# The SSD of a hybrid encoder trunk: decay as one exponent, states ahead of heads, no priority

## Chip, cores, metric

The kernel runs on one core of a Trainium2 chip. Its time is the device time of one execution in microseconds. The engines are named as the profile names them: PE (TensorE; PEld its weight loads), DVE (VectorE), ACT (ScalarE), POOL (GpSimd), and SP, which issues the DMAs.

## What is computed

A trunk of two layers on a sequence of L = 512 tokens and D = 1024 channels. Each layer normalises x, projects it, runs four mixers side by side (a bidirectional Mamba-2 SSD, a bidirectional RWKV-7 and two attentions), projects their 2048 channels back to 1024 and adds the result to x. The part that the change touches is the SSD, per direction:

```python
def _ssd(x, dt, A, bm, cm):
    xdt = chunk(x * dt[..., None])
    a = jnp.moveaxis(chunk(dt * A), -1, 1)
    a_cum = jnp.cumsum(a, axis=-1)
    scores = jnp.einsum("bclhn,bcshn->bhcls", cm, bm) * jnp.exp(_segsum(a))
    y_diag = jnp.einsum("bhcls,bcshp->bclhp", scores, xdt)
    decay_states = jnp.moveaxis(jnp.exp(a_cum[..., -1:] - a_cum), 1, -1)
    states = jnp.einsum("bclhn,bclhp->bchpn", bm, xdt * decay_states[..., None])
    ...
    y_off = jnp.einsum("bclhn,bchpn->bclhp", cm, states) * state_decay_out[..., None]
    return y_diag + y_off

y = y_f + y_b + xs * d_skip
```

There are 8 heads of 64 channels in two groups of four, which share B and C; chunks are of 128 tokens, so there are 4 of them and 3 state steps per direction. y is gated with silu(z) and normalised per group.

## The kernel before

`trunk` runs the layers one after the other. In a layer, `rwkv` runs first, with the attentions woven in. Then come the SSD (`ssd`), with work of others woven in, and the output projection, in two halves hf of 512 output channels. Projections are matmuls in three passes of high and low parts (whi·hhi, whi·hlo, wlo·hhi): a weight tile wf is loaded, ACT copies its high part (L153 in `split_w`), POOL subtracts for the low part (L154). `mm` (L82) issues every matmul, so PE's rows are told apart by tiles, not lines.

The names in `ssd`:

- The dt part works on 64 rows (2 directions of 32, of which 8 are heads). `sdt` is dt, `se` the running sum ac of dt·A within a chunk, `su` the decay to the chunk's end times dt (L738 to L747). Three PE transposes (pcx, L752) bring ac, dt and su into columns `colT` (L753); `exT` is exp(ac).
- `project(g)` makes, for group g, the convolved inputs: pjc (projection), craw (ACT L767), cacc (four DVE steps L772), cv (ACT tanh L774, DVE L775); then pjt for the gate zs; then transposes pxt to xs and bt (L793, L794) and pg to gT (L801), the product of C and B.
- Heads (L820 on): per head and direction, prow is a matmul that broadcasts ac over partitions; ACT takes four chunk ends, etot (L824); four DVE instructions subtract the column and take the minimum with a mask (L828); ACT takes exp (L831). Then per head 4 DVE products with dt (L837), 4 products with dt and sums (L838), one product with gT to mt (L841), and PE's yd, four matmuls. Two heads share one yd bank; ACT copies it to y (L849).
- States: three steps of POOL xd (L859), PE stp, and H on DVE (L864, or POOL L866 and DVE L869). Outputs: per chunk PE po, DVE of = po·exT (L881), POOL y += of (L884), POOL sk = xs·D (L888), DVE y += sk/2 (L890).
- Norm: y·zs (L893), squares jk on ACT (L897), rstd on DVE (L134) and POOL (L136), zs (L903).

The output projection adds 16 tiles kt of 128 mixer channels, 12 matmuls `mix` each per half. Kts 0 to 3 are the SSD's, 4 to 7 need no transposes, 8 to 15 are loaded (y) and transposed by PE (ytr L1251) into a "pj" bank, then split by ACT (yhi L1256) and DVE (ylo L1257). Weights are split at L1264 and L1265. The list `more` offers kts 4 to 15 of half 0 as fill work during group 1; kts 0 to 3 follow behind the SSD, and half 1 behind them.

What sets the order: the program is written in one order; a scheduler puts each engine's instructions in its own, by priority, which follows the program order, and `tc.high_priority()` raises everything issued while `urgent` is open. `with usual(): fill(...)` closes it for woven work. PSUM banks are 2 for "pj", 2 for "g" (pcx, prow, yd, stp, po, pxt, pg), 1 for "ga" and 3 for "mix".

Of the kernel before, what the change touches and what calls it, by code (L numbers as in the profile page):

```python
# [19 lines left out]
L = 512  # L20
# [11 lines left out]
F_S1 = 0.54  # L32
# [43 lines left out]
def trunk(ctx: ExitStack, tc: tile.TileContext, x_in, win, wwd, wdt, wout, w2a, cols, rows, sscal, consts, out, dbg=None,  # L76
# [4 lines left out]
    def mm(o, lhsT, rhs, start, stop, skip=False):  # L81
        PE.matmul(o, lhsT, rhs, start=start, stop=stop, skip_group_check=skip)  # L82
# [610 lines left out]
    def ssd(i, lay, ps, sp, op, yA, fill, more):  # L693
# [13 lines left out]
            G.tensor_tensor(w[:, :, 1, :], wf[:, h], w.bitcast(F32)[:, :, 0, :], op=ALU.subtract)  # L707
            ws.append(w.rearrange("p k a n -> p k (a n)"))
        fill.settle()
        urgent.enter_context(tc.high_priority())  # L710
        pd = ps.tile([128, L], F32, tag="pj", name="pjd")
        for k in range(8):
            mm(pd, ws[k // 4][:, k % 4, :], hT["hi"][:, k, :], k == 0, False)
# [31 lines left out]
                            op=ALU.subtract)  # L745
        S.activation(dec, dec, AF.Exp)
        V.tensor_tensor(dec, dec, dt, op=ALU.mult)  # L747
        colT = sp.tile([128, 3, 4, 64], F32, tag="colT", name="colT")
        for n, src in enumerate((ac, dt, dec)):
            pcx = ps.tile([128, 4, 64], F32, tag="g", name="pcx")  # L750
# [56 lines left out]
        for g in range(2):  # L807
            if g:
                fill.finish()
                fill.gens.extend(more)  # L810
            urgent.enter_context(tc.high_priority())
            cv, zs, xs, bt, gT = (gr[g][n] for n in ("cv", "zs", "xs", "bt", "gT"))

            etot = sp.tile([128, 2, 4, 4], F32, tag="etot", name="etot")
            y = sp.tile([128, 4, 256], F32, tag="y", name="y")
            yd = None
            for h in range(4):
                ex = []
                for d in range(2):
                    ri = d * 8 + 4 * g + h  # L820
                    pr = ps.tile([128, L], F32, tag="g", name="prow")
                    mm(pr, selE[:, ri:ri + 1].to_broadcast([128, 128]), acs, True, True)
                    p4 = pr.rearrange("p (c t) -> p c t", c=4)
                    S.activation(etot[:, d, :, h:h + 1], p4[:, :, 127:128] if d == 0 else p4[:, :, 0:1], AF.Exp)  # L824
                    ar = sp.tile([128, 4, 128], F32, tag="ar", name="ar", bufs=2)
                    row = 32 * d + 4 * g + h
                    for ch in range(4):
                        V.scalar_tensor_tensor(ar[:, ch, :], p4[:, ch, :], colT[:, 0, ch, row:row + 1],  # L828
                                               mneg[:, d * 128:d * 128 + 128],
                                               op0=ALU.subtract, op1=ALU.min)  # L830
                    S.activation(ar, ar, AF.Exp)  # L831
                    ex.append(ar)
                    with usual():
                        fill(F_S1)
                for ch in range(4):
                    row = 4 * g + h
                    V.tensor_scalar(ex[0][:, ch, :], ex[0][:, ch, :], colT[:, 1, ch, row:row + 1], None, op0=ALU.mult)  # L837
                    V.scalar_tensor_tensor(ex[1][:, ch, :], ex[1][:, ch, :], colT[:, 1, ch, row + 32:row + 33],  # L838
                                           ex[0][:, ch, :], op0=ALU.mult, op1=ALU.add)
                mt = sp.tile([128, 4, 128], F32, tag="mt", name="mt", bufs=2)  # L840
                V.tensor_tensor(mt, ex[1], gT, op=ALU.mult)  # L841
                with usual():
                    fill(F_S2)
                if h % 2 == 0:
                    yd = ps.tile([128, 4, 2, 64], F32, tag="g", name="yd")
                for ch in range(4):
                    mm(yd[:, ch, h % 2, :], mt[:, ch, :], xs[:, ch, h * 64:h * 64 + 64], True, True)
                if h % 2 == 1:
                    S.activation(y[:, :, (h - 1) * 64:(h + 1) * 64], yd.rearrange("p c h v -> p c (h v)"), AF.Copy)  # L849

            H = [[None] * 4, [None] * 4]
            for step in range(3):
                stp = ps.tile([128, 2, 256], F32, tag="g", name="stp")
                for d in range(2):
                    ch = step if d == 0 else 3 - step
                    nx = ch + 1 if d == 0 else ch - 1
                    row = 32 * d + 4 * g
                    xd = sp.tile([128, 4, 64], F32, tag="xd", name="xd", bufs=2)
                    G.tensor_tensor(xd, xs[:, ch, :].rearrange("p (h v) -> p h v", h=4),  # L859
                                    colT[:, 2, ch, row:row + 4].unsqueeze(2).to_broadcast([128, 4, 64]), op=ALU.mult)  # L860
                    mm(stp[:, d, :], bt[:, ch, :], xd.rearrange("p h v -> p (h v)"), True, True)
                    hn = sp.tile([128, 256], F32, tag=f"H{d}{step}", name="H")
                    if step == 0:
                        V.tensor_copy(hn, stp[:, d, :])  # L864
                    else:
                        G.tensor_tensor(hn.rearrange("p (h v) -> p h v", h=4),  # L866
                                        H[d][ch].rearrange("p (h v) -> p h v", h=4),
                                        etot[:, d, ch, :].unsqueeze(2).to_broadcast([128, 4, 64]), op=ALU.mult)
                        V.tensor_tensor(hn, hn, stp[:, d, :], op=ALU.add)  # L869
                    H[d][nx] = hn  # L870
                with usual():
                    fill(F_S3)
            for ch in range(4):
                po = ps.tile([128, 2, 256], F32, tag="g", name="po")
                ds = [d for d in range(2) if H[d][ch] is not None]
                for d in ds:
                    mm(po[:, d, :], cv[6 + g][:, ch * 128:ch * 128 + 128], H[d][ch], True, True)
                of = sp.tile([128, 2, 256], F32, tag="of", name="of", bufs=2)
                for d in ds:
                    row = 32 * d + 4 * g  # L880
                    V.tensor_tensor(of[:, d, :].rearrange("p (h v) -> p h v", h=4),  # L881
                                    po[:, d, :].rearrange("p (h v) -> p h v", h=4),
                                    exT[:, ch, row:row + 4].unsqueeze(2).to_broadcast([128, 4, 64]), op=ALU.mult)
                    G.tensor_tensor(y[:, ch, :], y[:, ch, :], of[:, d, :], op=ALU.add)  # L884
                with usual():
                    fill(F_S4)
# [12 lines left out]
            with usual():  # L899
                fill(F_S5)  # L900
# [453 lines left out]
def _consts():  # L1354
# [17 lines left out]
    c[:, C_MNEG + 128:C_MNEG + 256] = np.where(p[:, None] >= p[None, :], 0.0, -1e30)  # L1372
# [102 lines left out]
```

## Time and profile before

| | |
|---|---|
| median of 3 runs | 1831.52 us (1824.56 to 1835.34) |
| the profiled execution | 1831.36 us |
| its span | 1829.6 us |
| PE, DVE, ACT, POOL busy | 88%, 61%, 45%, 38% of the span |
| first mix matmul of half 0 to the last, layer 1 | 745.1 to 870.3 us |

The profile is of one execution; times count from the start of its span. A busy share is a share of time in which the engine has an instruction in work, and PE counts as busy at half clock as well; the granted clock of a stretch stands in the windows' column PEclk, 1.00 being 2.4 GHz.

### The profile page before, as it was taken

The page shows a single profiled execution, that of the slowest core. Times are in us where ns is not written, and L with a number is a line of the kernel's source. Part 1 is how long each engine was busy: PE and PEld are TensorE (multiplying, and loading weights), DVE is VectorE, ACT ScalarE, POOL GpSimd, SP SyncE. Part 2 cuts the span into 40 slices and gives each one's busy share as a digit, 9 for nine tenths or more (in the row PEclk, how much of TensorE's full clock was granted, in tenths as well). Part 3 has the DMA queues.
Part 4 walks back from the last instruction along what each step waited for, and adds up shares of the span by engine and source line. Part 5 has one row for each costly group of instructions (what it writes and reads, how often), then busy time and mean ns, then how long its engine had stood idle before and what let it go on. Part 6 is the DMA issues. An engine that isn't in the chain of part 4 may idle for free. (4 is left out here: it accounts for less than half of the span.)

```text
span 1829.6 us, 36888 instructions
## 1 busy us (share of the span) xinstructions
PE 1606.7 (88%) x15232; PEld 1347.2 (74%) x15232; DVE 1109.3 (61%) x2130; ACT 819.4 (45%) x1602; POOL 694.2 (38%) x708
## 2 busy tenths in 40 slices
PE   7898989998999979956988989899989999699478
PEld 6777877887878858844777777678778787588356
DVE  3567477486566357754256765865866763677632
ACT  4655436436435354521347463264274353554222
POOL 4554334243434125233455443342425251343223
PEclk9999988998999989976999999899979999899679
DMA  4211101110101132300431111011101010323013
GB/s 148 79 64 38 46 15 62 36 36 31 53 24 48 48 104 81 122 23 35 132 102 63 64 34 48 24 50 33 50 13 65 30 59 31 107 79 115 12 46 121
DMA packets 57512, 108.50 MB, mean 59 GB/s; under 512 B 6784, under 2 KB 8704, under 8 KB 57344
## 3 DMA queue, kind: packets, MB, share of 16 engines
q1 hardware_dynamic: 57344, 106.15, 17.4%
q8 instruction: 119, 1.95, 0.4%
q14 instruction: 49, 0.40, 0.1%
HBM read 95.64 MB, written 10.49 MB: 58 GB/s over the span
## 5 line engine op out<-in xcount | busy, mean ns | idle before, releaser
L154 POOL TENSOR_TENSOR wlo<-wf,whi 128x512 fp32r<-128x512 f32 x228 | 317.0, 1397 | 346.8 <-ACT whi L153 301.4
L82 PE MATMUL pjt<-whi,hhi 128*128 128x256 f32 x960 | 287.3, 300 | 7.8 <-ACT raw L279 3.3
L82 PE MATMUL pjt<-whi,hlo 128*128 128x256 f32 x960 | 285.0, 297 | 0.0
L82 PE MATMUL pjt<-wlo,hhi 128*128 128x256 f32 x960 | 283.2, 296 | 0.0
L82 PEld LDWEIGHTS pjt<-whi,hhi 128*128 128x128 f32 x960 | 189.6, 198 | 25.0 <-issue 10.7
L153 ACT ACTIVATE whi<-wf 128x512 fp32r<-128x512 f32 x228 | 141.3, 626 | 137.7 <-DMA wf<-in_win_dram 38.4
L82 PEld LDWEIGHTS pjt<-whi,hlo 128*128 128x128 f32 x960 | 189.9, 198 | 8.7 <-issue 7.5
L82 PEld LDWEIGHTS pjt<-wlo,hhi 128*128 128x128 f32 x960 | 189.6, 198 | 8.8 <-issue 7.7
L82 PE MATMUL pjc<-hhi,whi 128*128 128x512 f32 x384 | 158.7, 413 | 23.3 <-ACT raw L279 7.4
L82 PE MATMUL pjc<-hlo,whi 128*128 128x512 f32 x384 | 156.3, 407 | 0.0
L82 PE MATMUL pjc<-hhi,wlo 128*128 128x512 f32 x384 | 154.4, 410 | 0.9 <-POOL wlo L154 0.7
L82 PE MATMUL mix<-whi,yhi 128*128 128x512 f32 x256 | 93.6, 410 | 21.5 <-ACT yhi L1256 21.2
L915 ACT ACTIVATE p<-sc,nm 128x512 f32<-128x512 f32 x96 | 65.6, 684 | 97.0 <-DVE nm L912 66.1
L82 PEld LDWEIGHTS pjc<-hhi,whi 128*128 128x128 f32 x384 | 75.6, 197 | 42.6 <-ACT raw L279 8.4
L82 PE MATMUL mix<-whi,ylo 128*128 128x512 f32 x256 | 103.7, 405 | 0.0
L82 PE MATMUL mix<-wlo,yhi 128*128 128x512 f32 x256 | 100.4, 399 | 0.0
L82 PE MATMUL sc<-qT,qT 64*128 64x512 f32 (+1 forms) x256 | 92.9, 486 | 5.9 <-ACT y L1073 2.6
L912 DVE TENSOR_REDUCE nm<-sc 128x1 f32<-128x512 f32 x96 | 64.1, 691 | 46.7 <-PE sc L82 46.6
L82 PEld LDWEIGHTS pjc<-hhi,wlo 128*128 128x128 f32 x384 | 75.0, 195 | 22.8 <-POOL wlo L154 3.1
L1265 POOL TENSOR_TENSOR wlo<-wf,whi 128x512 fp32r<-128x512 f32 x32 | 42.6, 1333 | 122.9 <-ACT whi L1264 114.4
L82 PEld LDWEIGHTS pjc<-hlo,whi 128*128 128x128 f32 x384 | 75.5, 197 | 17.0 <-issue 1.7
L82 PE MATMUL ob<-v,ptS 128*128 128x128 f32 x512 | 78.8, 296 | 7.0 <-ACT ptS L939 6.9
(360 smaller groups left out, 3789.5 us busy)
## 6 DMA issues: line engine op xcount, KB each, us to landing
wf<-in_win_dram SPq DMA_DIRECT2D x224, 256.0 KB, 3.0
wf<-in_wout_dram SPq DMA_DIRECT2D x64, 256.0 KB, 2.7
y<-y_dram SPq DMA_DIRECT2D x24, 256.0 KB, 2.7
xt<-in_x_dram SPq DMA_DIRECT2D x8, 512.0 KB, 4.5
y_dram<-y SPq DMA_DIRECT2D x16, 256.0 KB, 2.5
y_dram<-rs SPq DMA_DIRECT2D x8, 256.0 KB, 2.0
x_dram<-t SPq DMA_DIRECT2D x8, 256.0 KB, 2.3
xt<-x_dram SPq DMA_DIRECT2D x4, 512.0 KB, 3.9
```

The costliest lines, as they stand in the source:

```text
L82: PE.matmul(o, lhsT, rhs, start=start, stop=stop, skip_group_check=skip)
L153: S.activation(hi, wf, AF.Copy)
L154: G.tensor_tensor(lo, wf, hi.bitcast(F32), op=ALU.subtract)
L912: V.tensor_reduce(nm, sc, axis=AX, op=ALU.max, negate=True)
L915: S.activation(p, sc, AF.Exp, bias=nm, accum_out=sm)
L1265: (V if kt % 2 else G).tensor_tensor(lo, wf, hi.bitcast(F32), op=ALU.subtract)
```

## The change

1. In the dt part, dt is bounded from below by 1e-37, ACT takes its logarithm, and ac − ln dt takes the place of dt in colT[:, 1]. A head's exponent subtracts that column, so that exp gives decay times dt at once. The mask is 1e30 where the pair counts (it was 0), so that the minimum no longer caps the exponent there.
2. The decay to the chunks' ends, etot, is made once: two DVE products, one matmul pe, one exp. dh = D/2 is made once.
3. In a group, the states come first, then the outputs, then the heads. y begins as xs·dh (POOL), outputs are added to it, then yd is added from its bank by DVE (two adds per group). A head has one DVE sum of 128x512 and one product with gT where it had eight small products and one product with gT.
4. yd takes a "pj" bank in group 1, "g" in group 0.
5. `urgent` and `usual` are gone from `ssd`.

```diff
-        urgent.enter_context(tc.high_priority())
         pd = ps.tile([128, L], F32, tag="pj", name="pjd")
...
         V.tensor_tensor(dec, dec, dt, op=ALU.mult)
+
+        V.tensor_scalar(dt, dt, 1e-37, None, op0=ALU.max)
+        S.activation(dt, dt, AF.Ln)
+        V.tensor_tensor(dt, ac, dt, op=ALU.subtract)
...
-        urgent.close()
+        ends = sp.tile([128, 4, 16], F32, tag="ends", name="ends")
+        ac4 = acs.bitcast(F32).rearrange("p (c t) -> p c t", c=4)
+        for d in range(2):
+            V.tensor_tensor(ends[:, :, 8 * d:8 * d + 8], ac4[:, :, 127 * (1 - d):128 - 127 * d].to_broadcast([128, 4, 8]),
+                            selE.bitcast(F32)[:, 8 * d:8 * d + 8].unsqueeze(1).to_broadcast([128, 4, 8]), op=ALU.mult)
+        pe = ps.tile([128, 4, 16], F32, tag="g", name="pe")
+        mm(pe, one.to_broadcast([128, 128]), ends, True, True)
+        etot = sp.tile([128, 4, 16], F32, tag="etot", name="etot")
+        S.activation(etot, pe, AF.Exp)
+        dh = sp.tile([128, 8], F32, tag="dh", name="dh")
+        V.tensor_scalar(dh, rws[:, R_D:R_D + 8], 0.5, None, op0=ALU.mult)
...
+            for step in range(3):
...
+            for ch in range(4):
+                po = ps.tile([128, 2, 256], F32, tag="g", name="po")
...
+                G.tensor_tensor(heads(y[:, ch, :]), heads(xs[:, ch, :]),
+                                dh[:, 4 * g:4 * g + 4].unsqueeze(2).to_broadcast([128, 4, 64]), op=ALU.mult)
...
+                    G.tensor_tensor(y[:, ch, :], y[:, ch, :], of[:, d, :], op=ALU.add)
...
             for h in range(4):
...
-                    S.activation(etot[:, d, :, h:h + 1], p4[:, :, 127:128] if d == 0 else p4[:, :, 0:1], AF.Exp)
...
-                        V.scalar_tensor_tensor(ar[:, ch, :], p4[:, ch, :], colT[:, 0, ch, row:row + 1],
+                        V.scalar_tensor_tensor(ar[:, ch, :], p4[:, ch, :], colT[:, 1, ch, row:row + 1],
...
-                for ch in range(4):
-                    row = 4 * g + h
-                    V.tensor_scalar(ex[0][:, ch, :], ex[0][:, ch, :], colT[:, 1, ch, row:row + 1], None, op0=ALU.mult)
-                    V.scalar_tensor_tensor(ex[1][:, ch, :], ex[1][:, ch, :], colT[:, 1, ch, row + 32:row + 33],
-                                           ex[0][:, ch, :], op0=ALU.mult, op1=ALU.add)
...
-                V.tensor_tensor(mt, ex[1], gT, op=ALU.mult)
+                V.tensor_tensor(mt, ex[0], ex[1], op=ALU.add)
+                V.tensor_tensor(mt, mt, gT, op=ALU.mult)
...
-                    yd = ps.tile([128, 4, 2, 64], F32, tag="g", name="yd")
+                    yd = ps.tile([128, 4, 2, 64], F32, tag="pj" if g else "g", name="yd")
...
-                    S.activation(y[:, :, (h - 1) * 64:(h + 1) * 64], yd.rearrange("p c h v -> p c (h v)"), AF.Copy)
+                    yh = y[:, :, (h - 1) * 64:(h + 1) * 64]
+                    V.tensor_tensor(yh, yd.rearrange("p c h v -> p c (h v)"), yh, op=ALU.add)
...
-                sk = sp.tile([128, 256], F32, tag="sk", name="sk", bufs=2)
-                G.tensor_tensor(sk.rearrange("p (h v) -> p h v", h=4), xs[:, ch, :].rearrange("p (h v) -> p h v", h=4),
-                                rws[:, R_D + 4 * g:R_D + 4 * g + 4].unsqueeze(2).to_broadcast([128, 4, 64]), op=ALU.mult)
-                V.scalar_tensor_tensor(y[:, ch, :], sk, 0.5, y[:, ch, :], op0=ALU.mult, op1=ALU.add)
...
-    c[:, C_MNEG:C_MNEG + 128] = np.where(p[:, None] <= p[None, :], 0.0, -1e30)
+    c[:, C_MNEG:C_MNEG + 128] = np.where(p[:, None] <= p[None, :], 1e30, -1e30)
```

Without the priority the order of PE's work is another. Before, in layer 1, this stands on PE from the end of the 144 mix matmuls of kts 4 to 15 to the mix of kt 0:

```order
L82 MATMUL mix<-wlo,yhi 128x512
L82 MATMUL stp<-xd,bt 128x256
L82 MATMUL po<-H,cv 128x256 x6
L793 MATMUL pxt<-cst,cv 128x128 x12
L82 MATMUL pg<-cv 128x128 x4
L82 MATMUL prow<-acs,cr 128x512 x2
L1251 MATMUL ytr<-cst,zs 128x128 x8
L82 MATMUL yd<-xs,mt 128x64 x4
L82 MATMUL prow<-acs,cr 128x512 x3
...
L82 MATMUL stp<-xd,bt 128x256 x2
...
L82 MATMUL stp<-xd,bt 128x256 x4
L82 MATMUL po<-H,cv 128x256 x6
```

Of the change, the same stretch on PE begins behind the 48 mix matmuls of kts 4 to 7 and ends with the mix of kt 8:

```order
L82 MATMUL mix<-wlo,yhi 128x512
L82 MATMUL prow<-acs,cr 128x512 x2
L82 MATMUL yd<-xs,mt 128x64 x4
L82 MATMUL prow<-acs,cr 128x512
...
L808 MATMUL pxt<-cst,cv 128x128 x8
...
L82 MATMUL pg<-cv 128x128 x4
L82 MATMUL stp<-xd,bt 128x256 x6
L82 MATMUL po<-H,cv 128x256 x6
L82 MATMUL prow<-acs,cr 128x512 x4
L82 MATMUL yd<-xs,mt 128x64 x4
...
L1253 MATMUL ytr<-cst,y 128x128 x4
L82 MATMUL mix<-whi,yhi 128x512 x4
```

Group 0's last three heads moved behind the first 36 mix matmuls, its stp and po (not in these rows) ahead of them, between the projections of group 1; the 96 mix matmuls of kts 8 to 15, with their ytr, moved behind group 1's third head.

On ACT, in the dt part of layer 1, before (su is the decay to the chunk's end, colT its columns):

```order
L153 ACTIVATE whi<-wf 128x512
L753 ACTIVATE colT<-pcx 128x256 x2
L755 ACTIVATE exT<-colT 128x256
L153 ACTIVATE whi<-wf 128x512 x2
L774 ACTIVATE cv<-cacc 128x512
L767 ACTIVATE craw<-pjc 128x512
```

and of the change:

```order
L756 ACTIVATE colT<-pcx 128x256
L758 ACTIVATE exT<-colT 128x256
L153 ACTIVATE whi<-wf 128x512 x2
L749 ACT_TABLE_LOAD
L749 ACTIVATE sdt<-sdt 64x512
L789 ACT_TABLE_LOAD
L789 ACTIVATE cv<-cacc 128x512
L782 ACTIVATE craw<-pjc 128x512
```

The logarithm (L749) stands ahead of a convolution's tanh (L789, L774 before), with a table load on either side.

## Rows read from the trace of the kernel before

**Rows 1.** The page: span, part 1, one group of part 5.
```profile
span 1829.6 us, 36888 instructions
...
PE 1606.7 (88%) x15232; PEld 1347.2 (74%) x15232; DVE 1109.3 (61%) x2130; ACT 819.4 (45%) x1602; POOL 694.2 (38%) x708
...
L154 POOL TENSOR_TENSOR wlo<-wf,whi 128x512 fp32r<-128x512 f32 x228 | 317.0, 1397 | 346.8 <-ACT whi L153 301.4
```
**Rows 2.** Windows, layer 1: length; PE, PEld, DVE, ACT, POOL busy; PEclk, DMA, GB/s.
```profile
745.00:787.50 42.50, 42.50 (x217) 35.63 (x216) 26.34 (x66) 18.00 (x33) 12.62 (x15) 1.00 0.39 119
787.50:855.40 67.90, 31.84 (x107) 21.53 (x105) 39.68 (x109) 14.03 (x41) 20.65 (x30) 0.61 0.07 24
855.40:870.30 14.90, 14.76 (x57) 11.64 (x57) 4.77 (x8) 4.30 (x9) 2.58 (x2) 0.81 0.12 36
```
**Rows 3.** Windows, the middle stage of layer 2.
```profile
1694.70:1762.80 68.10, 32.28 (x108) 21.80 (x106) 39.53 (x109) 14.12 (x41) 20.68 (x30) 0.62 0.07 23
```
**Rows 4.** Timeline of PE: start, us, what, [idle before <-releaser].
```profile
745.07 0.39 PE L82 MATMUL mix<-whi,yhi 128*128 128x512 f32 x1
...
788.38 3.17 PE L82 MATMUL po<-H,cv 128*128 128x256 f32 x12 [0.58 <-DVE H L869]
...
806.90 0.78 PE L82 MATMUL prow<-acs,cr 128*128 128x512 f32 x1
...
821.36 1.94 PE L82 MATMUL yd<-xs,mt 128*128 128x64 f32 x8 [4.14 <-DVE mt L841]
...
828.02 1.19 PE L82 MATMUL stp<-xd,bt 128*128 128x256 f32 x2 [1.90 <-DVE ar L828]
...
839.80 4.86 PE L82 MATMUL po<-H,cv 128*128 128x256 f32 x12 [0.58 <-DVE H L869]
855.39 2.07 PE L82 MATMUL mix<-whi,yhi 128*128 128x512 f32 x4 [10.72 <-ACT yhi L1256]
857.26 0.63 PE L82 MATMUL mix<-whi,ylo 128*128 128x512 f32 x1
857.68 0.63 PE L82 MATMUL mix<-wlo,yhi 128*128 128x512 f32 x1
```
**Rows 5.** Timeline of PE at the start of group 0's gate projection.
```profile
694.02 0.58 PE L82 MATMUL pjt<-whi,hhi 128*128 128x256 f32 x1 [1.49 <-ACT craw L767]
```
**Rows 6.** Timeline of ACT in the dt part.
```profile
672.07 1.28 ACT L722 ACT_TABLE_LOAD   x1
673.36 0.63 ACT L722 ACTIVATE sl<-su 64x512 f32<-64x512 f32 x1
...
692.86 0.63 ACT L774 ACTIVATE cv<-cacc 128x512 f32<-128x512 f32 x1 [3.29 <-DVE cacc L772]
693.39 0.58 ACT L767 ACTIVATE craw<-pjc 128x512 f32<-128x512 f32 x1
```
**Rows 7.** Timeline of DVE: the dt part, then heads of group 1.
```profile
683.83 0.42 DVE L738 TENSOR_SCALAR sdt<-sdt 64x512 f32<-64x512 f32 x1
...
689.63 1.74 DVE L747 TENSOR_TENSOR su<-su,sdt 64x512 f32<-64x512 f32 x1
...
798.39 2.15 DVE L828 SCALAR_TENSOR_TENSOR ar<-prow,colT,mneg 128x128 f32<-128x128 f32 x8
...
804.38 0.68 DVE L841 TENSOR_TENSOR mt<-ar,gT 128x512 f32<-128x512 f32 x1
...
809.80 0.87 DVE L837 TENSOR_SCALAR ar<-ar,colT 128x128 f32<-128x128 f32 x4 [0.76 <-ACT ar L831]
...
812.47 1.14 DVE L838 SCALAR_TENSOR_TENSOR ar<-ar,colT 128x128 f32<-128x128 f32 x4 [0.76 <-ACT ar L831]
...
830.66 0.67 DVE L841 TENSOR_TENSOR mt<-ar,gT 128x512 f32<-128x512 f32 x1
```
**Rows 8.** Timeline of PE: transposes of two successive kts.
```profile
765.39 0.60 PE L1251 MATMUL ytr<-cst,y 128*128 128x128 f32 x4
...
768.59 0.60 PE L1251 MATMUL ytr<-cst,y 128*128 128x128 f32 x4
```

More of the change, by code (lines that the diff above doesn't have):

```diff
@@ L810, in ssd @@
                 fill.gens.extend(more)
-            urgent.enter_context(tc.high_priority())
             cv, zs, xs, bt, gT = (gr[g][n] for n in ("cv", "zs", "xs", "bt", "gT"))
-            etot = sp.tile([128, 2, 4, 4], F32, tag="etot", name="etot")
+            heads = lambda t: t.rearrange("p (h v) -> p h v", h=4)
             y = sp.tile([128, 4, 256], F32, tag="y", name="y")
+            H = [[None] * 4, [None] * 4]
+            for step in range(3):
+                stp = ps.tile([128, 2, 256], F32, tag="g", name="stp")
+                for d in range(2):
+                    ch = step if d == 0 else 3 - step
+                    nx = ch + 1 if d == 0 else ch - 1
+                    row = 32 * d + 4 * g
+                    xd = sp.tile([128, 4, 64], F32, tag="xd", name="xd", bufs=2)
+                    G.tensor_tensor(xd, heads(xs[:, ch, :]),
+                                    colT[:, 2, ch, row:row + 4].unsqueeze(2).to_broadcast([128, 4, 64]), op=ALU.mult)
+                    mm(stp[:, d, :], bt[:, ch, :], xd.rearrange("p h v -> p (h v)"), True, True)
+                    hn = sp.tile([128, 256], F32, tag=f"H{d}{step}", name="H")
+                    if step == 0:
+                        V.tensor_copy(hn, stp[:, d, :])
+                    else:
+                        er = 8 * d + 4 * g
+                        G.tensor_tensor(heads(hn), heads(H[d][ch]),
+                                        etot[:, ch, er:er + 4].unsqueeze(2).to_broadcast([128, 4, 64]), op=ALU.mult)
+                        V.tensor_tensor(hn, hn, stp[:, d, :], op=ALU.add)
+                    H[d][nx] = hn
+                fill(F_S3)
@@ new lines, in ssd @@
+            for ch in range(4):
+                po = ps.tile([128, 2, 256], F32, tag="g", name="po")
+                ds = [d for d in range(2) if H[d][ch] is not None]
+                for d in ds:
+                    mm(po[:, d, :], cv[6 + g][:, ch * 128:ch * 128 + 128], H[d][ch], True, True)
+                G.tensor_tensor(heads(y[:, ch, :]), heads(xs[:, ch, :]),
+                                dh[:, 4 * g:4 * g + 4].unsqueeze(2).to_broadcast([128, 4, 64]), op=ALU.mult)
+                of = sp.tile([128, 2, 256], F32, tag="of", name="of", bufs=2)
+                for d in ds:
+                    row = 32 * d + 4 * g
+                    V.tensor_tensor(heads(of[:, d, :]), heads(po[:, d, :]),
+                                    exT[:, ch, row:row + 4].unsqueeze(2).to_broadcast([128, 4, 64]), op=ALU.mult)
+                    G.tensor_tensor(y[:, ch, :], y[:, ch, :], of[:, d, :], op=ALU.add)
+                fill(F_S4)
@@ L832, in ssd @@
                     ex.append(ar)
-                    with usual():
-                        fill(F_S1)
-                for ch in range(4):
-                    row = 4 * g + h
-                    V.tensor_scalar(ex[0][:, ch, :], ex[0][:, ch, :], colT[:, 1, ch, row:row + 1], None, op0=ALU.mult)
-                    V.scalar_tensor_tensor(ex[1][:, ch, :], ex[1][:, ch, :], colT[:, 1, ch, row + 32:row + 33],
-                                           ex[0][:, ch, :], op0=ALU.mult, op1=ALU.add)
+                    fill(F_S1)
                 mt = sp.tile([128, 4, 128], F32, tag="mt", name="mt", bufs=2)
-                V.tensor_tensor(mt, ex[1], gT, op=ALU.mult)
-                with usual():
-                    fill(F_S2)
+                V.tensor_tensor(mt, ex[0], ex[1], op=ALU.add)
+                V.tensor_tensor(mt, mt, gT, op=ALU.mult)
+                fill(F_S2)
                 if h % 2 == 0:
-                    yd = ps.tile([128, 4, 2, 64], F32, tag="g", name="yd")
+                    yd = ps.tile([128, 4, 2, 64], F32, tag="pj" if g else "g", name="yd")
                 for ch in range(4):
@@ L848, in ssd @@
                 if h % 2 == 1:
-                    S.activation(y[:, :, (h - 1) * 64:(h + 1) * 64], yd.rearrange("p c h v -> p c (h v)"), AF.Copy)
[L851 to L886, printed above, removed]
-                sk = sp.tile([128, 256], F32, tag="sk", name="sk", bufs=2)
-                G.tensor_tensor(sk.rearrange("p (h v) -> p h v", h=4), xs[:, ch, :].rearrange("p (h v) -> p h v", h=4),
-                                rws[:, R_D + 4 * g:R_D + 4 * g + 4].unsqueeze(2).to_broadcast([128, 4, 64]), op=ALU.mult)
-                V.scalar_tensor_tensor(y[:, ch, :], sk, 0.5, y[:, ch, :], op0=ALU.mult, op1=ALU.add)
@@ L898, in ssd @@
             r = rstd(sp, ss, 4, 1.0 / 256, EPS)
-            with usual():
-                fill(F_S5)
+            fill(F_S5)
             yA[g] = zs
@@ L905, in ssd @@
             tap("ya", yA[g], lambda a: a[:, g * 256:g * 256 + 256].rearrange("(c p) v -> p c v", p=128))
-            urgent.close()
     def softmax_rows(sc, ap):
@@ L1370, in _consts @@
     c[:, C_I64:C_I64 + 64] = (s[:, None] == np.arange(64)[None, :])
-    c[:, C_MNEG:C_MNEG + 128] = np.where(p[:, None] <= p[None, :], 0.0, -1e30)
-    c[:, C_MNEG + 128:C_MNEG + 256] = np.where(p[:, None] >= p[None, :], 0.0, -1e30)
+    c[:, C_MNEG:C_MNEG + 128] = np.where(p[:, None] <= p[None, :], 1e30, -1e30)
+    c[:, C_MNEG + 128:C_MNEG + 256] = np.where(p[:, None] >= p[None, :], 1e30, -1e30)
     n = np.arange(512)
```

## The prediction

> **What bounds the kernel now.** I read the page's totals first: the profiled execution took 1831.36 us, its span 1829.6, so 1.76 us lie around the span. It stands 0.16 us below the median of the three runs, so a sum against it can be set beside the median as it is. PE is busy 88% of the span [rows 1], which says that PE sets the time where it runs at full clock, and that the place to look for a gain is where it does not. So I cut the stretch that the change touches into stages, by windows. In layer 1 the 144 mix matmuls of kts 4 to 15 run from 745.07 [rows 4] to 787.5 with PE busy all the time at a granted clock of 1.00 (2.4 GHz); from 787.5 to 855.4, where group 1's SSD stands alone, PE is busy 31.84 of 67.90 us at a mean clock of 0.61, DVE 39.68, ACT 14.03, POOL 20.65; from 855.4 to 870.3 the last 48 mix matmuls of the first half (kts 0 to 3) follow at 0.81 [rows 2]. Layer 2 repeats the middle stage within 0.3 us, at 0.62 [rows 3]; one of its windows stands for three alike. No engine is full in the 68 us: it is a chain from PE to DVE to ACT to DVE to PE. Its parts are in the timeline of PE: outputs of group 0 from 788.38, the heads of group 1 with prow and yd, its states from 828.02, its outputs from 839.80, then 10.72 us of PE idle for norm and gate until mix goes on at 855.39 [rows 4]. These 68 us per layer are what the change can win from. Both halves of the work stay the same in PE matmuls, so I follow one clock: when the last mix matmul of the first half ends, 870.3 now.
>
> **The change part by part, for one layer.** Its largest effect is in the order rows of PE: where 144 mix matmuls stood ahead of group 1's SSD, 48 do; the 96 of kts 8 to 15 come behind group 1's heads, and group 1's states and outputs come ahead of its heads.
>
> *The logarithm.* It lies on a path that PE waits on: ACT does cv and craw before PE's pjt can begin [rows 5, 6]. Now DVE ends su at 691.4 [rows 7]; after that come the two small ends (0.15 each, 32 elements where a subtract of 128 takes 0.27), one cacc (0.7, as a product of 128x512) and the new max (0.42, as sdt) [rows 7], to 692.85. Ln 0.63 gives 693.5; the load of the table that tanh needs, 1.28, gives 694.8; cv 0.63 and craw 0.5 on give 696.1 [rows 6]. pjt began at 694.02 [rows 5]: **+2.1 us**. The other table load, ahead of Ln, lies in ACT's idle time ahead of cv, 3.29 us [rows 6]; if that were gone it would cost 1.28 more. That a load costs 1.28 and no more is read from two neighbours: the load at 672.07 ends at 673.35, and sl begins at 673.36 [rows 6]. The Trainium skill ("ScalarE: Activation LUTs", section "What ACT_TABLE_LOAD costs") gives some 1.38 us more for a drain at each switch; by it the two switches would add 2.8 us per layer and the time below would be some 5.5 us longer, an estimate from that page. The rows here do not agree with it, and I go by the rows.
>
> *etot, dh, the dropped small instructions.* 16 small exps and sk become one exp and one matmul; ACT and POOL have idle time in every stage of [rows 2], so beyond their place in a head (next but one) I count nothing.
>
> *PE work pulled ahead of mix.* 12 stp and po of group 0 now stand between projections, each 0.53 by the six po of 788.38 (3.17 us [rows 4]), in which waits for banks lie; I take half, 0.27, and keep 0.53 as the upper bound: +3.2. Three prow (0.23, as a mix matmul) and one yd (0.5; 1.94 busy at half clock, in which its eight records overlap) of group 0 go behind: −1.2. Each of the 12 also waits in order for DVE or POOL. The nearest row is the 0.58 us by which po waits for H behind other matmuls [rows 4]. The lower bound is nothing (projections lie between the steps, several us each); the upper is 1 us at each, 12 us. I take 1.0, two such waits, since between most of them stand 4 to 29 projection matmuls. **+3.0 us.**
>
> So mix begins at 745.07 + 5.1 = 750.2, and its first 36 matmuls, 2.75 us per kt without transposes (3.20 with them, four of which take some 0.4 [rows 8]), end at 758.4. Call this M.
>
> *Heads of group 0 behind M.* A head now has 3.5 us of DVE: 8 subtract-and-min (2.15), one add and one product of 128x512 (0.68 each), where ×dt (0.87) and ×dt-and-add (1.14) stood, too [rows 7]. But yd holds one of the two "g" banks, so the prow of a head follow one another through the other: prow 0.78 at half clock, 1.1 on DVE, twice, then exp and its gap 0.76, add and product, yd (1.94 at half clock) [rows 4, 7]: 7 us with 12 mix and the transposes in between. Three of them: M+22.5 with yd of the first. pxt and the copies that states need: M+24.8.
>
> *States and outputs of group 1.* States took from 828.02 to the outputs at 839.80, 11.8 us, of which 1.1 lay behind a head's ×dt-and-add and product on DVE [rows 4, 7]: 10.7, to M+35.5. Outputs hold PE 4.86 us [rows 4]: first prow of group 1 at M+40.4. POOL's y = xs·dh replaces sk one for one and stays within these 15 us (POOL 0.6 each).
>
> *Heads of group 1.* yd lies in "pj" here, so prow has both banks and DVE is the limit: 2.15 + 0.68 + 0.68 and a gap of 0.76 for exp [rows 7] = 4.27 per head, against 8.76 now (26.28 us for three, from product to product [rows 7]). The first takes 6.0, the third's yd ends at M+55.8.
>
> *Mix behind it.* ytr and yhi: mix of kt 8 at M+57.5. PE comes out of the stage at half clock, as now at 855.39: two starts of mix stand 0.42 to 0.43 apart there [rows 4], so I take two kts at 12 × 0.43 = 5.2 us: M+67.9. The ten others at 3.20 us each, transposes included [rows 8]: M+99.9. The last head, y·zs, squares and zs of group 1 (most of the 10.72 us of idle PE now [rows 4]) lie under these 32 us. Kts 0 to 3, which need them, come last, some 25 us later; if that cover were gone, up to 10.7 us per layer would come back.
>
> **Sum.** First half ends at 758.4 + 99.9 = 858.3, against 870.3: −12.0 us per layer. Layer 2 has the same three stages [rows 3], so −24.0: 1831.4 − 24.0 = **1807.4 us**. The scheduler also reorders much small work in layer 2's RWKV; no row prices that, and I give it ±5 us.
>
> **The rivals.**
> *A, slower: the heads stay at the pace of now.* If the limit of a head is the round trip from prow to its bank's release, not DVE, then the dropped instructions buy nothing. For it: PE waits 1.90 us ahead of the first stp for DVE's ar, 4.14 ahead of a yd [rows 4]; against: DVE's ×dt rows stand between those subtracts now [rows 7] and vanish. Priced: three heads of group 1 at 8.76 instead of 4.27 (+13.5), three of group 0 at 8.76 instead of 7.0 (+5.3): 18.8 − 12.0 = +6.8 per layer, **1845 us**. Now those heads stand ahead of 96 matmuls with nothing of mix beside them, so each us counts fully. The loss begins where a head takes 2.0 us more than forecast over all six.
> *B, no change: the moved stp and po stall PE.* Each of 12, waiting about 1 us in order behind POOL's xd, in a stage where PE is full today [rows 2]: +12 per layer, **1831 us**. For it: the priority is gone, and POOL there has wlo of 1.4 us each in its queue [rows 1]; against: matmuls of projections lie between.
> *C, faster: Ln is covered and group 0's heads run at 4.5 us, too* (mix between them covers the round trips): −2.1 and −5 more per layer, **1793 us**.
> *D, as the forecast, but kts 8 to 15 pace slower,* since their y come in two buffers and their transposes share "pj" with yd: 4.2 us instead of 3.20 for eight, +8 per layer, **1823 us**; at 4.7 the gain is gone.
>
> **How the numbers follow.** A measurement here tells 0.5% from no change, 9.2 us: faster is below 1822.4, slower above 1840.7. Chances: forecast 0.56, C 0.12, D 0.08 (half of it on either side of the bound), B 0.11, A 0.13. Faster 0.56 + 0.12 + 0.04 = 0.72; same 0.11 + 0.04 = 0.15; slower 0.13. The forecast's own range is 1795 to 1821 (the bounds of the in-order waits upward, C's terms by half downward). The range that holds 8 in 10 goes from 1786 (C, with layer 2's 5 us) to 1837 (B and D whole, little of A).
>
> **What would show it.** Right: mix of kts 4 to 6 ends near 758; between group 1's first prow and its third yd some 15 us; no idle time of PE over 2 us behind the first mix of kt 8; the stage at half clock is about 50 us and not 68. Table loads of 1.28 with no gap behind. Wrong: products of one head to the next at 8 us or more (A); PE idle summed over 10 us between 694 and 750 with stp or po behind it (B); ytr late by loads of y (D). If the projections of group 1 slow down as a whole, the cause is none of these.

## The result, and the profile after

| | before | changed |
|---|---|---|
| median | 1832.52 us (4 runs, 1824.56 to 1835.34) | 1805.47 us (4 runs, 1803.19 to 1807.17) |
| ratio | | 0.9858, 95% interval 0.9838 to 0.9877 |
| span of the profiled execution | 1829.6 us | 1804.1 us |

The changed kernel is faster by 1.4%; 1807 us had been forecast. The page of the changed kernel, against [rows 1]: PE is busy a little longer and DVE 41 us less.

```profile
span 1804.1 us, 36754 instructions
...
PE 1614.5 (89%) x15236; PEld 1354.8 (75%) x15236; DVE 1068.2 (59%) x2020; ACT 819.6 (45%) x1570; POOL 700.6 (39%) x708
```

The three stages of layer 1, against [rows 2] (windows; columns as there): 36 mix matmuls, then the stage with the heads, then the mix of kts 8 to 15 and 0 to 2.

```profile
751.30:759.50 8.20, 8.20 (x38) 6.75 (x37) 4.49 (x9) 3.13 (x6) 2.22 (x2) 1.00 0.34 106
759.50:819.30 59.80, 36.67 (x132) 26.40 (x131) 35.74 (x92) 14.66 (x29) 15.12 (x22) 0.66 0.03 12
819.30:857.40 38.10, 37.20 (x180) 30.56 (x181) 16.71 (x25) 14.21 (x29) 7.49 (x6) 0.95 0.39 132
```

The timeline of PE, against [rows 4, 5], with the points at which the prediction puts a time:

```profile
694.51 0.58 PE L82 MATMUL pjt<-whi,hhi 128*128 128x256 f32 x1 [0.59 <-ACT craw L782]
...
751.30 0.40 PE L82 MATMUL mix<-whi,yhi 128*128 128x512 f32 x1
...
759.55 1.00 PE L82 MATMUL yd<-xs,mt 128*128 128x64 f32 x8
...
781.12 1.81 PE L82 MATMUL yd<-xs,mt 128*128 128x64 f32 x8
...
785.51 0.60 PE L82 MATMUL stp<-xd,bt 128*128 128x256 f32 x2
...
802.38 0.94 PE L82 MATMUL prow<-acs,cr 128*128 128x512 f32 x2 [0.15 <-DVE of L862]
...
807.26 1.97 PE L82 MATMUL yd<-xs,mt 128*128 128x64 f32 x8 [1.56 <-DVE mt L886]
...
811.51 1.97 PE L82 MATMUL yd<-xs,mt 128*128 128x64 f32 x8 [1.31 <-DVE mt L886]
...
815.76 1.97 PE L82 MATMUL yd<-xs,mt 128*128 128x64 f32 x8 [1.32 <-DVE mt L886]
...
819.26 2.07 PE L82 MATMUL mix<-whi,yhi 128*128 128x512 f32 x4 [0.69 <-ACT yhi L1258]
...
861.46 0.50 PE L82 MATMUL mix<-whi,yhi 128*128 128x512 f32 x1
```

The last row is the first mix matmul of half 1; before, it stood at 870.26. To compare kernels whose layers lie at different times, I cut every trace at the same four events, from its PE timeline. **A** goes from the start of the RWKV's last yb row (645.24 here) to the first mix. **B** goes from there to the end of half 0, taken as the start of the layer's last mix less 44.0 us, which half 1 takes in both kernels (870.26 to 914.29 before, 861.46 to 905.48 now). **R** goes from layer 1's last mix to the last yb row of layer 2. A + B is the SSD with its surroundings; R holds nothing that the change touches. In layer 2 of changed, e1, e4, e5, e7, e9 and e13 the last eight yb matmuls stand in two rows, 0.8 to 1.7 us apart, and the event is the second; cut at the first, A there would be longer and R shorter by as much (changed: 103.0 and 634.2). Each kernel was profiled once, and executions of one kernel lie up to 16 us apart (the kernel before, beside e14: 1824.92 to 1840.89); no trace here shows in which stretch. Changed and e1 agree within 0.1 us in A + B, but a difference of a few us counts only where both layers show it.

| kernel | A, B layer 1 | A + B | A, B layer 2 | A + B | R | median, us |
|---|---|---|---|---|---|---|
| before | 99.4, 125.2 | 224.6 | 96.9, 125.5 | 222.4 | 641.2 | 1832.5 |
| changed | 106.1, 110.2 | 216.3 | 101.7, 109.8 | 211.5 | 635.5 | 1805.5 |
| e1, priority back | 107.0, 109.4 | 216.4 | 102.4, 109.1 | 211.5 | 654.5 | 1824.5 |
| e2, before without priority | 96.8, 124.7 | 221.5 | 97.9, 123.9 | 221.8 | 643.0 | 1833.1 |
| e4, changed with heavy heads | 102.9, 115.8 | 218.7 | 101.9, 114.4 | 216.3 | 645.2 | 1815.8 |
| e5, changed with yd in "g" | 105.9, 112.3 | 218.2 | 101.3, 111.6 | 212.9 | 644.8 | 1819.4 |
| e7, before with yd in "pj" | 99.4, 112.1 | 211.5 | 98.8, 112.5 | 211.3 | 635.5 | 1799.4 |
| e8, before with light heads | 101.8, 119.5 | 221.3 | 98.2, 119.5 | 217.7 | 643.2 | 1823.6 |
| e9, both | 101.7, 109.2 | 210.9 | 97.8, 109.8 | 207.6 | 635.7 | 1797.3 |
| e12, changed, heads first | 104.1, 100.1 | 204.2 | 101.8, 100.0 | 201.8 | 638.5 | 1785.5 |
| e13, e12 with early logarithm | 100.8, 100.1 | 200.9 | 102.2, 100.2 | 202.4 | 637.4 | 1782.5 |
| e14, e13 with group 0's yd in "ga" | 103.5, 88.4 | 191.9 | 103.5, 88.0 | 191.5 | 645.1 | 1772.8 |

The 25.5 us of the span come from three places: the SSD of layer 1 (8.3), the SSD of layer 2 (10.9), and 5.7 us in layer 2's RWKV, whose code is the same and whose instructions stand in another order; the other 0.4 us lie ahead of them. So the SSD gave 19.2 us where 24 had been forecast, and the sum came out by a gift of 5.7. (With layer 2 cut at the first yb row these are 17.9 and 7.0.)

### The profile page after: what moved, and what is told of

It is laid out like the page before. It is cut to its first block, busy times and chain, and to the rows that moved or that the text cites. A ratio compares the mean times of both kernels' runs of the same rounds, so it can differ in the third digit from the quotient of the medians.

```text
span 1804.1 us, 36754 instructions
## 1 busy us (share of the span) xinstructions
PE 1614.5 (89%) x15236; PEld 1354.8 (75%) x15236; DVE 1068.2 (59%) x2020; ACT 819.6 (45%) x1570; POOL 700.6 (39%) x708
## 4 chain that ended last, share of the span: by engine, by line
PE 56%; DVE 25%; ACT 9%; issue 5%; POOL 3%; DMA 2%; POOLq 0%; SPq 0%; ACTq 0%; DVEq 0%
PE pjt L82 11%; PE pjc L82 11%; PE mix L82 8%; PE sc L82 3%; PE ob L82 3%; DVE sv L571 1%; PE p L82 1%; PE pa L82 1%; PE ph L82 1%; DVE sv L573 1%; PE pp L82 1%; PE ptp L939 1%; DVE gqk L971 1%; DVE ar L878 1%; PE pje L82 1%
## 5 line engine op out<-in xcount | busy, mean ns | idle before, releaser
L82 PE MATMUL mix<-whi,ylo 128*128 128x512 f32 x256 | 101.7, 397 | 0.0
L82 PEld LDWEIGHTS pjc<-hlo,whi 128*128 128x128 f32 x384 | 76.6, 199 | 17.9 <-issue 2.5
```

## The experiments

**e1: the priority again.** Edit: `urgent.enter_context(tc.high_priority())`, `urgent.close()` and `with usual():` at their old places in the changed `ssd`.

> The changed kernel with the scheduler's priority put back at its old places in the SSD. Theory 'cover' (the gain comes from where the 96 mix matmuls of kts 8 to 15 stand, which the bank of group 1's yd decides): the order of PE in the SSD is the same but for one matmul, so the time from the first mix to the end of half 0 stays at 110 us per layer and the total at 1803 to 1809. Rival 'priority' (dropping it is what freed the order): back towards 1820 or more.

Measured: 1824.53 us, 0.9965 of before (0.9949 to 0.9982). A + B is what the changed kernel has, within 0.1 us in both layers. So putting the priority back did nothing to this kernel's SSD, and the sentence ahead of the order rows, "Without the priority the order of PE's work is another", was wrong about the cause. The total lies where the rival 'priority' puts it, but not in the stages that the rival means: the 19 us between this kernel and the changed one lie in R, 654.5 against 635.5. Of them 13.5 are lost in one stretch of layer 2's RWKV, between the pm matmuls of its first and its second unit (155.3 and 304.7 us behind layer 1's last mix, where the changed kernel has 155.2 and 291.1). The longest wait of PE in it: a transpose pqt stands ahead of projections that then run without a wait, and waits for DVE, which has a chain of its own to finish. The row on PE, and the windows around it:

```profile
1183.67 1.11 PE L959 MATMUL pqt<-cst,qk 128*128 128x128 f32 x4 [6.96 <-DVE qT L964]
```

```profile
1170.00:1180.00 10.00, 6.44 (x53) 5.80 (x50) 9.93 (x19) 5.48 (x11) 7.27 (x6) 0.97 0.28 95
1180.00:1190.00 10.00, 6.33 (x30) 6.22 (x30) 4.30 (x4) 1.12 (x2) 1.28 (x1) 0.52 0.03 11
```

PE waits 7 us, and in the window of the wait's end the granted clock is 0.52, mostly the 1.2 GHz level. In the changed kernel the longest such wait of this stretch is 2.58 us. Nothing in the diff speaks of this place.

**e2: the kernel before without the priority.** Edit: the same lines taken out of the `ssd` of before.

> The kernel before without the priority in the SSD, nothing else changed. If the priority does nothing to the SSD itself, as putting it back into the changed kernel showed, A + B stays at 222 to 226 per layer, and whatever the total does beyond that shows in layer 2's RWKV, whose order is another (641 us before, 635 to 655 in the runs so far): total 1823 to 1845. Rival: priority held the SSD's order back, A + B under 220.

Measured: 1833.06 us, ratio 1.0012 (0.9995 to 1.0029); A + B 221.5 and 221.8, just below the expected band. Dropping the priority is worth 3.1 and 0.6 us of A + B in this kernel, and nothing in the total.

**e5: group 1's yd back in "g".**

```diff
-                    yd = ps.tile([128, 4, 2, 64], F32, tag="pj" if g else "g", name="yd")
+                    yd = ps.tile([128, 4, 2, 64], F32, tag="g", name="yd")
```

> The changed kernel with group 1's yd in a 'g' bank, as before; by the order of PE, all 144 mix matmuls of kts 4 to 15 then stand ahead of group 1's states again. Theory 'cover': the norm and gate of group 1 (10.7 us) and its last head are bare again, about 15 us per layer lost, minus what the mix hides of group 0's heads: 1815 to 1825. Rival 'lighter heads': the heads carry the gain in either order and the total stays at 1803 to 1809.

Measured: 1819.43 us, 0.9931 of before (0.9907 to 0.9955). The order of PE did go back: the mix of kts 8 to 15 stands ahead of group 1's SSD again. So it is the bank that moves them. By the code, ytr takes "pj" banks as well, and so shares them with yd. But the total fell into the band of 'cover' for another reason: A + B is only 1.9 and 1.4 us above the changed kernel, and 9.3 us come from R. By the stages, then, the changed kernel keeps most of its gain in either order, as the rival said. My reading, argued and not shown: with states first, what the bank would let mix hide stands bare anyway. The yd of group 1, on PE:

```profile
818.15 1.94 PE L82 MATMUL yd<-xs,mt 128*128 128x64 f32 x8 [4.13 <-DVE mt L886]
...
826.10 1.97 PE L82 MATMUL yd<-xs,mt 128*128 128x64 f32 x8 [1.32 <-DVE mt L886]
...
832.22 1.94 PE L82 MATMUL yd<-xs,mt 128*128 128x64 f32 x8 [3.62 <-DVE mt L886]
...
840.16 1.97 PE L82 MATMUL yd<-xs,mt 128*128 128x64 f32 x8 [3.39 <-DVE mt L886]
```

A light head takes 7.3 us here (22.01 for three; long and short ones alternate, as before), against 4.25 in the changed kernel.

**e4: the heavy heads in the changed kernel.** Edit: the logarithm out, colT[:, 0] in the exponent and the masks at 0 again, and per head

```diff
-                V.tensor_tensor(mt, ex[0], ex[1], op=ALU.add)
-                V.tensor_tensor(mt, mt, gT, op=ALU.mult)
+                for ch in range(4):
+                    V.tensor_scalar(ex[0][:, ch, :], ex[0][:, ch, :], colT[:, 1, ch, row:row + 1], None, op0=ALU.mult)
+                    V.scalar_tensor_tensor(ex[1][:, ch, :], ex[1][:, ch, :], colT[:, 1, ch, row + 32:row + 33],
+                                           ex[0][:, ch, :], op0=ALU.mult, op1=ALU.add)
+                V.tensor_tensor(mt, ex[1], gT, op=ALU.mult)
```

> The changed kernel with the heads of before (products with dt, four and four small DVE instructions per head, no logarithm), all else as changed. Theory 'lighter heads': each of six heads per layer that nothing covers gets 1.3 us longer (0.87 + 1.14 - 0.68), 8 us per layer less 0.5 for the logarithm, so 1805 + 15 = 1820; the stage between the 36 mix matmuls and the mix of kt 8 goes from 59.7 to 67 us. Rival 'cover alone': the heads wait for banks anyway, under 2 us per layer, 1809 at most.

Measured: 1815.81 us, 0.9931 of before (0.9908 to 0.9954). The profiled execution took 1823.14 us, 7.3 more than the median; in it R is 9.7 us longer than in the changed kernel, and A + B 2.4 and 4.8, which is more than the medians differ by (10.3). As far as this trace goes, the heavy heads cost less than the 7.5 expected and more than the 2 of the rival. The yd of group 1:

```profile
807.80 1.97 PE L82 MATMUL yd<-xs,mt 128*128 128x64 f32 x8 [2.00 <-DVE mt L887]
...
812.49 1.97 PE L82 MATMUL yd<-xs,mt 128*128 128x64 f32 x8 [1.77 <-DVE mt L887]
...
817.71 1.97 PE L82 MATMUL yd<-xs,mt 128*128 128x64 f32 x8 [2.29 <-DVE mt L887]
```

A heavy head with two banks for prow takes 5.0 us (9.91 for two), 0.7 more than a light one in the changed kernel. There the lighter DVE work is worth 0.7 us per head, and by e5 the second bank 3.1.

**e7: one word in the kernel before**, group 1's yd in "pj" (the diff of e5, upside down).

> The kernel before with one word changed: group 1's yd takes a 'pj' bank. By the order of PE, the 96 mix matmuls of kts 8 to 15 then come behind group 1's third head, and the states and outputs of group 1 lie among them. Theory 'cover': a large part of the gain or more comes with this word alone, 845 to 862 for the end of half 0 in layer 1 and 1785 to 1815 in total. Rival 'lighter heads': the heads at 8.8 us stand bare ahead of mix and nothing is gained, 1825 to 1835.

Measured: 1799.41 us, 0.9828 of before (0.9794 to 0.9862), the end of half 0 in layer 1 at 855.0. A + B falls by 13.1 and 11.1 us, more than by the whole change. The rival is out: the heads are bare ahead of mix here, but on two banks, and group 1's states, outputs and norm lie among the mix of kts 8 to 15. Its first and third yd of group 1 stand 9.52 us apart, 4.8 us per heavy head where [rows 7] has 8.76:

```profile
789.79 1.97 PE L82 MATMUL yd<-xs,mt 128*128 128x64 f32 x8 [4.23 <-DVE mt L841]
...
799.31 0.90 PE L82 MATMUL yd<-xs,mt 128*128 128x64 f32 x3 [1.84 <-DVE mt L841]
```

The word does two things at once, the pace of the heads and the place of mix, and no run here separates them.

**e8: the logarithm and the light heads in the kernel before**, all else as it was. The edit is the diff's dt part, masks and head loop.

> The kernel before with the logarithm and the light heads alone (order of the program, priority, bank of yd and etot as before). I look at two stretches of layer 1: A, end of the RWKV to the first mix (before 99.4 us), and B, first mix to the end of half 0 (before 125.2, changed 110.2). Theory 'light heads': four heads of group 1 lose 1.3 us of DVE and some waiting each, B 117 to 120, A 99 to 101, total 1815 to 1820 if layer 2's RWKV keeps its 641 us. Rival 'cover alone': B stays over 123, total 1828 or more.

Measured: 1823.57 us, 0.9955 of before (0.9939 to 0.9970). B is 119.5 in both layers, as expected, A 101.8 and 98.2, on either side of its band; A + B falls by 3.3 and 4.7. The total lies 3.6 us above its band, of which R, 643.2 instead of 641.2, explains 2.0. The first and the fourth yd of group 1, 7.9 us per light head on one bank:

```profile
802.23 1.94 PE L82 MATMUL yd<-xs,mt 128*128 128x64 f32 x8
...
825.85 1.81 PE L82 MATMUL yd<-xs,mt 128*128 128x64 f32 x8
```

**e9: e8 and the word of e7 together.**

> The kernel before with the logarithm, the light heads and group 1's yd in 'pj': the changed kernel less its states ahead of the heads, its one etot and its dropped priority. Theory 'states first costs': PE is not stopped between projections by stp and po, and group 1's states and outputs lie under mix, so A 99 to 101 and B 106 to 109 (112.1 with the heavy heads, less four heads of 1.3), A + B 207 against 216.3 of the changed kernel; total 1785 to 1800, with 10 us either way by the order of layer 2's RWKV. Rival 'states first pays': A + B 216 or more.

Measured: 1797.32 us, 0.9803 of before (0.9777 to 0.9829); A + B 210.9 and 207.6, 5.4 and 3.9 us below the changed kernel, though A and B each lie at or a little above their bands in layer 1. The light heads add 0.6 and 3.7 us to the bank. The first and the third yd of group 1, 4.6 us per light head on two banks:

```profile
792.96 1.97 PE L82 MATMUL yd<-xs,mt 128*128 128x64 f32 x8 [2.88 <-DVE mt L840]
...
802.17 1.97 PE L82 MATMUL yd<-xs,mt 128*128 128x64 f32 x8 [1.70 <-DVE mt L840]
```

Before, e7, e8 and e9 make a square of bank and heads, all else in the program being equal. One bank: heavy 8.8, light 7.9. Two banks: heavy 4.8, light 4.6. The second bank is worth 3.3 to 4.0 us per head, the lighter DVE work 0.9 on one bank and 0.2 on two.

**e12: the changed kernel with the heads ahead of the states again.** Edit: the loops over `step` and `ch` moved behind the loop over `h`, and ahead of it

```diff
+            for ch in range(4):
+                G.tensor_tensor(heads(y[:, ch, :]), heads(xs[:, ch, :]),
+                                dh[:, 4 * g:4 * g + 4].unsqueeze(2).to_broadcast([128, 4, 64]), op=ALU.mult)
```

> The changed kernel with one move: the heads stand ahead of the states and outputs again, y still begun as xs*dh, all else as changed. It differs from the changed kernel by the order of these blocks alone. Theory 'states first costs': A falls from 106.1 to 99 to 102 and B from 110.2 to 105 to 109. Rival 'etot, the accumulation or the missing priority cost': A + B stays at 213 to 217.

Measured: 1785.51 us, 0.9741 of before (0.9708 to 0.9774). This one move is worth 12.1 and 9.7 us of A + B: in layer 1 A fell by no more than 2.0, to 104.1, above the expected band, and B to 100.1, below it. So in the changed kernel "states first" costs these 10 to 12 us. In the changed kernel's timeline of PE, states and outputs of group 1 stand bare from 785.51 to 802.38, 16.9 us. In this kernel the same stp stand among mix, with no wait worth a note:

```profile
799.36 1.06 PE L82 MATMUL stp<-xd,bt 128*128 128x256 f32 x2
...
804.53 0.60 PE L82 MATMUL stp<-xd,bt 128*128 128x256 f32 x2
...
810.35 0.60 PE L82 MATMUL stp<-xd,bt 128*128 128x256 f32 x2
```

**e13: the logarithm early.** Edit, in e12:

```diff
         V.scalar_tensor_tensor(dt, xb, 0.0, ln, op0=ALU.max, op1=ALU.add)
+        V.tensor_scalar(ln, dt, 0.125, 1e-37, op0=ALU.mult, op1=ALU.max)
+        S.activation(ln, ln, AF.Ln)
...
-        V.tensor_scalar(dt, dt, 1e-37, None, op0=ALU.max)
-        S.activation(dt, dt, AF.Ln)
-        V.tensor_tensor(dt, ac, dt, op=ALU.subtract)
+        V.tensor_tensor(ln, ac, ln, op=ALU.subtract)
...
-        for n, src in enumerate((ac, dt, dec)):
+        for n, src in enumerate((ac, ln, dec)):
```

> As the run before it, with the logarithm taken right after dt is there instead of after the decay. If the logarithm sits on the path ahead of pjt, as the prediction has it (2.1 us), A gets 1 to 2 us shorter; if it is hidden, A stays within 0.5 us.

Measured: 1782.53 us, 0.9717 of before (0.9684 to 0.9751). A is 3.3 us shorter in layer 1 and 0.4 longer in layer 2, and the intervals of e12 and e13 overlap: whether it pays stays open.

**e14: e13 with group 0's yd in a bank of its own.**

```diff
-                    yd = ps.tile([128, 4, 2, 64], F32, tag="pj" if g else "g", name="yd")
+                    yd = ps.tile([128, 4, 2, 64], F32, tag="pj" if g else "ga", name="yd")
```

> The run with the heads first and the early logarithm, and one word more: group 0's yd takes the bank 'ga', which the attention has left free, where it had one of the two 'g' banks. If group 0's heads are held by the single bank left to prow (7 us per head in the prediction), they now fit between the projections and its last states between the first mix matmuls, so that A + B falls from 201 to 190 or 195 per layer and the total to 1760 to 1775. If DVE or the wait for yd holds them, A + B stays over 198.

Measured: 1772.82 us, 0.9705 of before (0.9681 to 0.9729), the fastest of all; A + B 191.9 and 191.5, as expected. Three of group 0's heads now fit between the projections, the fourth stands among the first mix matmuls. R is 645.1 here against 637.4 in e13, which takes part of the 19.9 us of A + B back. The stages of layer 1:

```profile
746.60:765.00 18.40, 17.20 (x78) 13.31 (x76) 12.55 (x23) 4.16 (x7) 11.81 (x13) 1.00 0.28 85
765.00:787.00 22.00, 13.57 (x58) 10.43 (x58) 18.06 (x50) 9.25 (x21) 8.53 (x11) 0.69 0.04 13
787.00:835.00 48.00, 45.74 (x220) 37.46 (x219) 22.06 (x41) 15.89 (x34) 17.84 (x21) 0.97 0.34 111
```

The stage in which the SSD stands bare is 22 us long, where it was 59.8 in the changed kernel and 67.9 before [rows 2].

## Why the prediction came out, and what in it did not

Point by point, for layer 1; M is the end of the first 36 mix matmuls.

| step | forecast | measured |
|---|---|---|
| pjt starts | +2.1 | +0.49 (694.51) |
| pjt to first mix | +3.0 | +5.7 (56.79 against 51.05) |
| M | 758.4 | 759.55 |
| states of group 1 start | M+24.8 | M+26.0 |
| its first prow | M+40.4 | M+42.8 |
| one head of group 1 | 4.27 | 4.25 (807.26, 811.51, 815.76) |
| mix of kt 8 | M+57.5 | M+59.7 |
| end of half 0 | M+99.9 | M+101.9 |
| the layer | −12.0 | −8.8 |

*The logarithm was too dear.* The load ahead of Ln lies in idle time, as said, and Ln itself starts 1.5 us earlier than reckoned: DVE comes to su 2.3 us sooner than before [rows 7] (0.4 of it because the RWKV ends earlier), of which a cacc of 1.80 us (not 0.7) gives a part back. On DVE and ACT:

```profile
687.36 1.74 DVE L746 TENSOR_TENSOR su<-su,sdt 64x512 f32<-64x512 f32 x1
...
689.23 1.80 DVE L787 SCALAR_TENSOR_TENSOR cacc<-craw,cols,cacc 128x512 f32<-128x512 f32 x1
690.96 0.41 DVE L748 TENSOR_SCALAR sdt<-sdt 64x512 f32<-64x512 f32 x1
```

```profile
687.19 1.28 ACT L749 ACT_TABLE_LOAD   x1
691.40 0.63 ACT L749 ACTIVATE sdt<-sdt 64x512 f32<-64x512 f32 x1 [2.93 <-DVE sdt L748]
692.05 1.28 ACT L789 ACT_TABLE_LOAD   x1
693.35 0.63 ACT L789 ACTIVATE cv<-cacc 128x512 f32<-128x512 f32 x1
```

The second load begins 0.02 us after Ln ends and cv 0.02 us after the load: 1.28 us per switch and nothing more. The Trainium skill ("ScalarE: Activation LUTs", section "What ACT_TABLE_LOAD costs") adds a drain of about 1.38 us; no row here shows one.

*The work pulled ahead of mix was too cheap.* This is the step that failed in layer 1: "I take half, 0.27". The waits in order, priced 1.0, hardly came: from 694.51 on PE waits 0.6 us in all, once, for a prow, and as much before. So B, "the moved stp and po stall PE", is out. What costs is PE itself, busy 56.17 us in that stretch and not 50.44, with 0.95 of the clock granted instead of 0.97 (0.05 × 56.8 is 2.8 us, 0.03 × 51.1 is 1.5): the half clock with which the stretch begins lasts until about 700 where it ended at about 697. An inserted pair of po looks like this:

```profile
743.06 0.28 PE L82 MATMUL pjt<-whi,hhi 128*128 128x256 f32 x1
743.17 1.02 PE L82 MATMUL po<-H,cv 128*128 128x256 f32 x4
743.85 0.47 PE L82 MATMUL pjt<-whi,hlo 128*128 128x256 f32 x1
744.15 0.28 PE L82 MATMUL pjt<-wlo,hhi 128*128 128x256 f32 x1
```

Two po hold PE 0.68 us, and the next pjt holds it 0.30 where others hold it 0.12. A single stp or po holds PE 0.24 (744.99 to 745.23), three in a row 1.11, and behind each the next pass takes 0.18 more: 0.43 for each of the twelve, 5.2 us where 3.2 had been reckoned. That is nearer to 0.53, kept as the upper bound, than to 0.27.

*The states of group 1 were 1.3 us too short.* From 785.51 to the first prow took 16.9 us, not 15.6. Group 0's norm is in the way: zs stands on DVE for 2.73 us between the states, and y = xs·dh on POOL for 2.33, while PE waits 2.82 and 2.59 us for xd.

```profile
787.48 1.02 POOL L136 TENSOR_TENSOR rstdr<-rstdv,cst 128x4 f32<-128x4 f32 x1
...
791.41 2.33 POOL L857 TENSOR_TENSOR y<-xs,dh 128x256 f32<-128x256 f32 x4 [0.82 <-DVE zs L906]
...
794.26 0.62 POOL L838 TENSOR_TENSOR xd<-xs,colT 128x256 f32<-128x256 f32 x1
```

*The heads were right in size, and half right in reason.* 4.27 had been worked out from DVE alone, and in the changed kernel DVE is the limit; its only idle time in a head is 0.70 us for ACT's exp:

```profile
802.94 2.16 DVE L878 SCALAR_TENSOR_TENSOR ar<-prow,colT,mneg 128x128 f32<-128x128 f32 x8 [0.18 <-PE prow L82]
805.79 0.69 DVE L885 TENSOR_TENSOR mt<-ar 128x512 f32<-128x512 f32 x1 [0.70 <-ACT ar L881]
806.52 0.69 DVE L886 TENSOR_TENSOR mt<-mt,gT 128x512 f32<-128x512 f32 x1
```

But the square of before, e7, e8 and e9 shows that the second bank does most of it (3.3 to 4.0 us of the fall from 8.76, against 0.2 to 0.9), and the prediction put the fall to the lighter DVE work and the bank together. Rival A named the limit of the kernel before rightly, "the round trip from prow to its bank's release", and overlooked that group 1's yd leaves that bank free, so its 8.76 us did not come. Group 0's heads, whose yd keeps a "g" bank, took 21.57 us for three (759.55 to 781.12) where 21 had been forecast. That is luck in part: the terms given for one add up to 7.8, not 7. The half of C by which they run at 4.5 did not come; it would have been worth 7.5 us per layer and not 5.

*Mix behind it* ran as forecast, 42.2 us against 42.4, and at 3.20 us per kt, so D is out too. But two errors offset each other there: the half clock lasted 3.6 us and not two kts, and things that had no price filled the rest, of which only kt 10's wait of 0.90 us for its yhi is read here. The stage at half clock, which "What would show it" puts at about 50 us, took 59.7; the prediction's own points give 57.5. The upper end of its own range, 1821, does not come out of its bounds either: 12 us of waits instead of 1.0 would be 22 us more for both layers.

*The sum over both layers* held for a reason that was not in it. "I give it ±5 us" stood for layer 2's RWKV; it gave 5.7, just beyond that. The kernels here show how little such a gift has to do with the edit: R lies between 635.5 and 654.5 us. e1 shows one place; why the order comes out as it does in each kernel was not tried and stays open, also for the 5.7 us.

*What the change is made of* can be read as a ladder of A + B, layer 1 and 2. Before to e7, the bank of yd: −13.1 and −11.1. To e9, the light heads: −0.6 and −3.7. To e12, one etot, y summed from the bank and no priority: −6.7 and −5.8. From e12 to the changed kernel, states first: +12.1 and +9.7. The sum is −8.3 and −10.9. So the largest gain sits in a word that the prediction uses for the heads of group 1 and does not price by itself, and one of the named parts of the change loses most of it again. The steps depend on their order: the bank is worth 10.4 and 10.1 us on top of the light heads (e8 to e9), but 1.9 and 1.4 where the states already stand first (e5). The third step holds three edits whose shares stay open; the priority alone, taken out of the kernel before, gave 3.1 and 0.6 (e2).

## What to carry to other kernels

When a stage is bare, ask first what moves other work under it and which buffer its round trip turns on; here one word, the bank of an accumulator, did more than eight small products taken out of each head (e7 against e8). Take a composite change apart before keeping it: without "states first", with the logarithm early and group 0's yd in a free bank, it is 1772.8 us instead of 1805.5. And where a scheduler orders the program anew, compare stages and not totals, since untouched code moved by up to 19 us.

## What the runs showed of the hardware

A plain fp32 matmul of 128x256 (stp, po) between the passes of a split projection costs PE 0.43 us at full clock in the changed kernel: alone it holds PE 0.24 us, two in a row 0.68, three 1.11, and the pjt pass behind them takes 0.30 us instead of 0.12. A switch of the activation table cost 1.28 us, with 0.02 us to the next instruction. A wait of 7 us on PE in e1 was followed by a window with 0.52 of the clock granted.
